# A GLA and stick-breaking hybrid layer: the first branch's output split where it is made, scores two blocks ahead, values one block behind, loads further ahead in the first pairs

## The chip, the cores and the metric

The kernel runs on one core of one Trainium2 chip, as one program. The metric is the device time of one execution in microseconds (us); the time before is the median of three executions, and a profile of one more execution shows where it goes. In the text PE is the matrix engine, PEld its weight loads, DVE the vector engine, ACT the scalar engine, POOL the GpSimd engine, and SP the engine whose queue issues nearly all DMAs.

## What is computed

One layer over 1024 tokens of width 1024, in float32. The reference, cut to what matters here:

```python
h = rmsnorm(x, norm_g)
proj = h @ w_in                                  # 9232 columns
(g_q, g_k, g_v, g_gate, g_rank, s_q, s_k, s_v, s_gate, m_logits) = jnp.split(proj, ...)
log_a = log_sigmoid(g_rank @ w_dec_up + b_dec) / 16
o_gla = gla_chunked(g_q, g_k, g_v, log_a)        # 4 heads, dk 128, dv 256
o_gla = rmsnorm(o_gla, gla_norm_g) * silu(g_gate)
y_a = o_gla @ w_pa
# stick-breaking, 8 heads, d 128, blocks of 128 queries against the causal prefix:
z = q @ k.T / sqrt(d); log1m = where(causal, log_sigmoid(-z), 0)
between = reverse_cumsum(log1m) - log1m
A = where(causal, exp(log_sigmoid(z) + between), 0);  o = A @ v
y_b = (o * silu(s_gate)) @ w_pb
x = x + (sigmoid_a * y_a + sigmoid_b * y_b) @ w_o;  return rmsnorm(x, final_g)
```

## The kernel before

Every product of float32 matrices is made of three matmuls of a reduced format (`F32R`): each operand is kept as a high part and a low part, and high x high, high x low and low x high are summed in PSUM. `split(src, hi, lo)` makes the parts: ACT copies `src` to `hi` (L161), DVE subtracts (L162). Arrays that a later stage needs go through DRAM (`d_...`).

The stages, in order: the norm of x and the first value projection; the other value projections; the **pairs stage**, in which `Pairs` runs 28 jobs of 7 units (12 matmuls of 512 columns each, a Strassen-like scheme) that project everything else but the second branch's gate; inside it, from unit 49 on, the **GLA stage**, which puts the first branch's small matmuls between the units; the **stick-breaking stage**; the projection of the second branch (`w_pb`) with the merge; and the output product.

*The first pairs.* In the first 22 units of `Pairs` the decay factors are made (`djobs`), in the next 27 (`tjobs`) the rows of `w_o` are loaded (`t_load`), combined by four subtractions on DVE (`t_sum`, L681) and stored (`t_store`, `d_t`). The recorded order of ACT and DVE is kept as written in the first 22 units (`manual_schedule`). In the other 27, and in the GLA and stick-breaking stages, a scheduler orders each engine's instructions by its own model of times. `gqk_pair` multiplies the GLA queries and keys with the decay factors `d_e`, which it loads (L523) at the moment of eviction.

*The GLA stage.* 32 steps (4 heads, 8 blocks of 128 tokens). `gl_gate` (L803) turns a block's output, multiplies it with its gate into `g` (two tiles of 128x128 side by side) and stores `g` in `d_ogl`, one array for each head.

*The stick-breaking stage.* `steps` are 8 heads of 8 blocks (h, i). `scores` (L878) multiplies a block's queries with the keys (`z`, up to 1024 columns in one or two PSUM banks, of which there are two), ACT makes two sigmoids of each bank (L898 into `eb`, L899 into `be`), DVE runs a product scan over the block on the diagonal (L902) and over the rest (L905) and multiplies (L910) into `be`. `turn` (L912) transposes `be` on PE, 128x128 at a time (L924), and splits the result into `ath`, `atl`. `values` (L929) multiplies two blocks' weights with the values (`av`, L940 to L942) in a single PSUM bank, multiplies with the gate (L943) and stores. The loop (L1018) does, for step s: load the queries of s + 2, load the next head's keys and values at i = 1, `scores` of s + 1, a unit of `st` if it stands there, `turn` of s, perhaps a unit, and `values` of the two blocks where i is odd. So PE meets `values` right behind the `turn` that it needs.

`st` is a line of units (24 matmuls of 512 columns each, `proj_t`, L200 to L202) that fill PE: three units a head (`SB_PLAN`), first the 16 units of the second branch's gate (`gate`), then the 16 of the first branch's output projection (`pa`). In between stands the reload of the first branch's output: `o_dma` loads 512 columns of one head of `d_ogl` into a `raw` tile (two buffers, which the weight loads use as well), and `o_split` splits them into `oq`, in the tiles that `hq` (the normed input) no longer needs. That is 16 `split`s of 128x512 on ACT and DVE, in two groups, in the fifth and sixth head.

All DMAs of these stages are issued by SP, in order; a DMA that has to wait for a buffer holds up those behind it.

Of the kernel before, what the change touches and what calls it, by code (L numbers as in the profile page):

```python
# [99 lines left out]
def hybrid_layer(ctx: ExitStack, tc: tile.TileContext, x, norm_g, w_in, w_up, b_dec,  # L100
# [20 lines left out]
    def dram_set(nm, count, shape, dt=F32):  # L121
        return [dram.tile(shape, dt, tag=f"{nm}{i}", name=f"d_{nm}{i}") for i in range(count)]
# [5 lines left out]
    d_gq, d_gk, d_e1, d_e2 = (dram_set(nm, GLA_H, [P, T]) for nm in ("gq", "gk", "e1", "e2"))  # L128
    d_gv = dram_set("gv", GLA_H, [P, NT, 2, DV])
    d_gg = dram_set("gg", GLA_H, [P, 2, T])  # L130
    d_ogl = dram_set("ogl", GLA_H, [P, 2, T])
    d_ga, d_gb, d_ma = (dram_set(nm, KB, [P, T]) for nm in ("ga", "gb", "ma"))
    d_a21 = dram_set("a21", 2, [P, 4, HALF])

# [29 lines left out]
    def half(n):  # L164
        return slice(n * HALF, (n + 1) * HALF)
# [57 lines left out]
        nc.gpsimd.tensor_tensor(r, r, nhalf, op=ALU.pow)  # L223


    def pair_job(w, c0, evict):

        t = {}

# [38 lines left out]
            nc.scalar.activation(t[nm], t[bank], AF.Copy)  # L268

        def unit(u):  # L270
            if u == 0:
                product("x", "B11", "A11", first=True)
                keep("s1", "x")
            elif u == 1:
                product("y", "B21", "A12", first=True)
                evict(0, 0, t["y"], t["s1"])
            elif u == 2:
                product("x", "T2", "S2")
                keep("s2", "x")
# [237 lines left out]
        return pair_job(w_in, c0 + i * DV, evict)  # L517

    def gqk_pair(c0, i, scale, d_e, dst):
        def evict(J, n, bank, add):  # L520
            h = 2 * i + J
            e = ev.tile([P, HALF], F32, tag="f", name="f")
            nc.sync.dma_start(e, d_e[h][:, half(n)])  # L523
            nc.vector.scalar_tensor_tensor(e, total(bank, add), scale, e, op0=ALU.mult, op1=ALU.mult)
            nc.sync.dma_start(dst[h][:, half(n)], e)

        return pair_job(w_in, c0 + i * DV, evict)

    def silu(v, dst):
        o = stage().bitcast(F32)  # L530
# [130 lines left out]
    for jobs in djobs:  # L661
        for fn, h in jobs:
            fn(h)
        pairs.run(1)
    manual.close()
    dq_ctx.close()


    wt = {}
    tq_ctx = ExitStack()  # L670
    tq = tq_ctx.enter_context(tc.tile_pool(name="tq", bufs=2, reuse_waits="tile"))

    def t_load(j):
        wt[j] = tq.tile([P, 4, HALF], F32, tag="t", name="t")
# [12 lines left out]
    for j in range(4):  # L687
        tjobs[5 * j].append((t_load, (j,)))
        for i in range(4):
            tjobs[5 * j + 4 + i].append((t_sum, (j, i)))  # L690
        tjobs[5 * j + 9].append((t_store, (j,)))
    for jobs in tjobs:
        pairs.run(1)
        for fn, args in jobs:
            fn(*args)
    tq_ctx.close()


# [104 lines left out]
    def gl_gate(h, b):  # L803
        t = gblk.pop((h, b))
        pt = ps.tile([P, HALF], F32, tag="tr", name="tr")
        for j in range(2):
            js = slice(j * P, (j + 1) * P)
            nc.tensor.transpose(pt[:, js], t["on"][:, js], ident)
        for j in range(2):
            js = slice(j * P, (j + 1) * P)  # L810
            nc.vector.scalar_tensor_tensor(t["g"][:, j], pt[:, js], vcol[:, 20 + j:21 + j], t["g"][:, j],
                                           op0=ALU.mult, op1=ALU.mult)
        nc.sync.dma_start(d_ogl[h][:, :, b * P:(b + 1) * P], t["g"])

    gl_half(0, 0)
    gl_load(*steps[0])
# [25 lines left out]
    def load_head(h):  # L842
        kts[h] = sl.tile([P, 2, T], F32R, tag="k", name="k")
        nc.sync.dma_start(kts[h].bitcast(F32), d_k[h])
        vts[h] = sl.tile([P, NT, 2, P], F32R, tag="v", name="v")
        nc.sync.dma_start(vts[h].bitcast(F32), d_v[h])

    def load_q(h, i):
        qts[h, i] = sl.tile([P, 2, P], F32R, tag="q", name="q", bufs=3)
# [1 line left out]

    steps = [(h, i) for h in range(SB_H) for i in range(NT)]
    load_head(0)
    for s in range(2):
        load_q(*steps[s])
    pairs.run()
    s_ctx.close()
# [13 lines left out]
    bets["first"] = sb.tile([P, T], F32, tag="be", name="be")  # L871
# [6 lines left out]
    def scores(h, i):  # L878
# [4 lines left out]
        om = ebuf[i % 2]  # L883
        be = bets.pop("first", None)
        if be is None:
            be = sb.tile([P, T], F32, tag="be", name="be")
        bets[h, i] = be
        npc = 1 if L <= HALF else 2
        w = L // npc
# [39 lines left out]
    def values(h, m):  # L929

        ath, atl = abuf[(m + 1) % 2]
        v = vts[h]
        gs = slice(m * DV, (m + 1) * DV)
        gate = ev.tile([P, HALF], F32, tag="f", name="f")[:, 0:DV]
        nc.sync.dma_start(gate, d_sg[h][:, gs])
        pav = ps.tile([P, HALF], F32, tag="av", name="av", bufs=1)
        ns = 2 * m + 2
        for s in range(ns):
            j = 2 * m + 1 - s
            nc.tensor.matmul(pav[:, 0:DV], v[:, j, 0], ath[:, s], start=s == 0, stop=False)  # L940
            nc.tensor.matmul(pav[:, 0:DV], v[:, j, 0], atl[:, s], start=False, stop=False)  # L941
            nc.tensor.matmul(pav[:, 0:DV], v[:, j, 1], ath[:, s], start=False, stop=s == ns - 1)  # L942
        nc.vector.tensor_mul(gate, pav[:, 0:DV], gate)  # L943
        nc.sync.dma_start(d_osb[h][:, gs], gate)

# [35 lines left out]
    def gate_load(h):  # L981
        return load(w_in, C_SG + h * P, ("g", h))
# [26 lines left out]
    line += [gate(5, 0), gate_load(7), gate(6, 0), o_dma(0, 0), gate(7, 0), o_dma(0, 1), o_split(0, 0), gate(5, 1),  # L1009
             o_dma(0, 2), o_split(0, 1), o_dma(0, 3), gate(6, 1), o_split(0, 2), pa_load(0), o_split(0, 3), pa_load(1),  # L1010
             gate(7, 1), o_dma(1, 0), pa_load(2), pa(0, 0), o_dma(1, 1), o_split(1, 0), o_dma(1, 2), pa(1, 0),
             o_split(1, 1), o_dma(1, 3), pa(2, 0), o_split(1, 2), o_split(1, 3)]
# [330 lines left out]
```

## Time and profile before

| what | us |
|---|---|
| median of 3 executions | 1249.28 (1249.15 to 1250.16) |
| the profiled execution | 1247.65 |
| its span, first to last instruction | 1245.8 |
| first pairs and decay, PE 74.66 busy | 125 to 200 |
| the stretch with the loads of `w_o`, PE 22.71 busy | 200 to 225 |
| GLA stage, PE 450.00 busy | 250 to 700 |
| stick-breaking stage, from its first score | 728 to 1028 |

A row of a view by lines names the source line, the engine, the operation, the output and the inputs, then the number of instructions, their busy time and the mean of one, and the idle time of the engine just ahead of them with what ended it. PE's busy time holds the tail of each matmul, since matmuls are pipelined: a row of 512 columns is shown with 0.39 us, while the next one starts 0.23 us later. How much PE does in a stretch is therefore read from starts, not from the busy share.

### The profile page before, as it was taken

The page shows a single profiled execution, that of the slowest core. Times are in us where ns is not written, and L with a number is a line of the kernel's source. Part 1 is how long each engine was busy: PE and PEld are TensorE (multiplying, and loading weights), DVE is VectorE, ACT ScalarE, POOL GpSimd, SP SyncE. Part 2 cuts the span into 40 slices and gives each one's busy share as a digit, 9 for nine tenths or more (in the row PEclk, how much of TensorE's full clock was granted, in tenths as well). Part 3 has the DMA queues.
Part 4 walks back from the last instruction along what each step waited for, and adds up shares of the span by engine and source line. Part 5 has one row for each costly group of instructions (what it writes and reads, how often), then busy time and mean ns, then how long its engine had stood idle before and what let it go on. Part 6 is the DMA issues. An engine that isn't in the chain of part 4 may idle for free. (4 is left out here: it accounts for less than half of the span.)

```text
span 1245.8 us, 17778 instructions
## 1 busy us (share of the span) xinstructions
PE 1214.7 (98%) x6339; PEld 1013.8 (81%) x6339; DVE 801.1 (64%) x1321; ACT 544.9 (44%) x1030; POOL 303.6 (24%) x304
## 2 busy tenths in 40 slices
PE   8999999999999999999999999999989999999997
PEld 8999887888888888888888887877777778888876
DVE  5475866746666576666744347787787876345576
ACT  5344663344334444444433334454554554332343
POOL 2495431414233232242232110000000000023201
PEclk9999999999999999999999999999999999999999
DMA  7554459836555465564643865354675535666653
GB/s 272 187 155 126 152 214 300 291 121 196 165 180 174 147 196 185 183 217 159 213 134 114 275 208 166 122 175 155 194 230 164 165 127 200 208 205 242 244 202 119
DMA packets 197460, 233.02 MB, mean 187 GB/s; under 512 B 12246, under 2 KB 143340, under 8 KB 194300
## 3 DMA queue, kind: packets, MB, share of 16 engines
q1 hardware_dynamic: 196796, 230.84, 56.3%
q8 instruction: 50, 0.82, 0.3%
q10 hardware_dynamic: 576, 1.05, 0.2%
q14 instruction: 38, 0.31, 0.1%
HBM read 145.34 MB, written 86.51 MB: 186 GB/s over the span
## 5 line engine op out<-in xcount | busy, mean ns | idle before, releaser
L299 DVE TENSOR_TENSOR f<-pp,f 128x512 f32<-128x512 f32 x84 | 57.9, 689 | 83.5 <-PE pp L264 80.7
L162 DVE TENSOR_TENSOR wl<-tt,wh 128x1024 fp32r<-128x1024 f32 x56 | 69.7, 1244 | 63.5 <-ACT wh L161 63.1
L162 DVE TENSOR_TENSOR wl<-raw,wh 128x1024 fp32r<-128x1024 f32 x55 | 79.6, 1448 | 37.0 <-ACT wh L161 35.9
L161 ACT ACTIVATE wh<-raw 128x1024 fp32r<-128x1024 f32 x55 | 58.0, 1057 | 89.2 <-PE pp L263 50.6
L161 ACT ACTIVATE wh<-tt 128x1024 fp32r<-128x1024 f32 x56 | 59.3, 1059 | 84.1 <-PE pp L263 83.6
L907 POOL TENSOR_SCALAR_AFFINE_SELECT be<-be 128x128 f32<-128x128 f32 x64 | 23.6, 369 | 280.6 <-ACT be L899 214.9
L236 POOL TENSOR_TENSOR tt<-raw 128x512 f32<-128x512 f32 x28 | 38.5, 1375 | 183.1 <-DVE wl L162 173.3
L268 ACT ACTIVATE f<-pp 128x512 f32<-128x512 f32 x84 | 49.6, 591 | 72.5 <-PE pp L264 67.5
L905 DVE TENSOR_TENSOR_SCAN eb<-eb 128x128 f32<-128x128 f32 (+6 forms) x56 | 71.8, 1282 | 6.3 <-ACT eb L898 4.0
L223 POOL TENSOR_TENSOR r<-r,nhalf 128x1 f32<-128x1 f32 x40 | 23.7, 593 | 207.8 <-DVE r L222 207.8
L898 ACT ACTIVATE eb<-z 128x384 f32<-128x384 f32 (+4 forms) x96 | 48.4, 505 | 41.7 <-PE z L896 28.4
L161 ACT ACTIVATE ath<-tr 128x512 fp32r<-128x512 f32 (+2 forms) x96 | 44.0, 496 | 37.2 <-PE tr L924 36.3
L162 DVE TENSOR_TENSOR atl<-tr,ath 128x512 fp32r<-128x512 f32 (+2 forms) x96 | 51.1, 546 | 6.6 <-ACT ath L161 6.6
L941 PE MATMUL av<-atl,v 128*128 128x256 f32 x160 | 46.9, 293 | 4.6 <-DVE atl L162 4.6
L200 PE MATMUL pp<-bh,wh 128*128 128x512 f32 x128 | 49.8, 389 | 0.0
L201 PE MATMUL pp<-bl,wh 128*128 128x512 f32 x128 | 49.8, 389 | 0.0
L202 PE MATMUL pp<-bh,wl 128*128 128x512 f32 x128 | 49.8, 389 | 0.0
L924 PE MATMUL tr<-ident,be 128*128 128x128 f32 x288 | 44.6, 278 | 5.2 <-DVE be L910 4.2
L910 DVE TENSOR_TENSOR be<-be,eb 128x128 f32<-128x128 f32 (+3 forms) x64 | 48.3, 755 | 2.1
L899 ACT ACTIVATE be<-z 128x384 f32<-128x384 f32 (+4 forms) x96 | 49.0, 512 | 0.0
L924 PEld LDWEIGHTS tr<-ident,be 128*128 128x128 f32 x288 | 32.8, 141 | 19.8 <-DVE be L910 9.9
L553 ACT ACTIVATE o<-o,vcol 128x512 f32<-128x512 f32 x32 | 23.2, 725 | 56.7 <-DMA o<-d_gb 40.8
(434 smaller groups left out, 4016.2 us busy)
## 6 DMA issues: line engine op xcount, KB each, us to landing
raw<-in_w_in_dram SPq DMA_DIRECT2D x31, 1024.0 KB, 6.0
d_v<-o SPq DMA_DIRECT2D x32, 256.0 KB, 3.0
d_gv<-o SPq DMA_DIRECT2D x32, 256.0 KB, 3.8
v<-d_gv SPq DMA_DIRECT2D x32, 256.0 KB, 3.1
d_q<-o SPq DMA_DIRECT2D x16, 512.0 KB, 3.9
d_k<-o SPq DMA_DIRECT2D x16, 512.0 KB, 5.1
k<-d_k SPq DMA_DIRECT2D x8, 1024.0 KB, 5.4
v<-d_v SPq DMA_DIRECT2D x8, 1024.0 KB, 7.5
```

The lines of the kernel that those rows point to most:

```text
L161: nc.scalar.activation(hi, src, AF.Copy)
L162: eng.tensor_sub(lo, src, hi.bitcast(F32))
L200: nc.tensor.matmul(pt, whi[:, kb], h_, start=kb == 0, stop=False)
L201: nc.tensor.matmul(pt, whi[:, kb], l_, start=False, stop=False)
L202: nc.tensor.matmul(pt, wlo[:, kb], h_, start=False, stop=kb == KB - 1)
L268: nc.scalar.activation(t[nm], t[bank], AF.Copy)
L299: nc.vector.tensor_add(add, bank, add)
L898: nc.scalar.activation(om[:, osl], zt[:, 0:w], AF.Sigmoid, scale=-inv_sqrt)
L899: nc.scalar.activation(be[:, osl], zt[:, 0:w], AF.Sigmoid, scale=inv_sqrt)
L905: nc.vector.tensor_tensor_scan(rest, rest, rest, om[:, T - P:T - P + 1], op0=ALU.mult, op1=ALU.min)
L910: nc.vector.tensor_mul(be[:, off:T], be[:, off:T], om[:, off + 1:T + 1])
L924: nc.tensor.transpose(pt[:, b * P:(b + 1) * P], be[:, c:c + P], ident)
```

## The change

1. `gl_gate` splits `g` as soon as it is made and stores both parts: `d_ogl` becomes two arrays, for the high and the low parts. `o_dma(n)` loads all four heads' 512 columns straight into `oq`, by four DMAs of 1 MB, and `o_split` is gone.
2. `scores` runs two blocks ahead of `turn` and not one; `be` has three buffers and not two; queries are loaded three steps ahead.
3. `values` of blocks 2m and 2m + 1 comes behind the `turn` of block 2m + 2, and the last of a head behind the first `turn` of the next.
4. A head's values are loaded as two halves; three halves fit (before, two heads).
5. In `tjobs` the sums stand two units later and the store too, with three buffers and not two; the decay factors of `gqk_pair` are loaded by `before(u)`, ahead of the unit's matmuls; the written order of ACT and DVE is kept up to the end of `tjobs`.

```diff
-    d_ogl = dram_set("ogl", GLA_H, [P, 2, T])
+    d_ogl = dram_set("ogl", 2, [P, 2, GLA_H, T])
...
         def unit(u):
+            if before:
+                before(u)
...
     def gqk_pair(c0, i, scale, d_e, dst):
+        es = {}
+
+        def before(u):
+            if u in (0, 3, 4, 5):
+                J, n = {0: (0, 0), 3: (1, 1), 4: (1, 0), 5: (0, 1)}[u]
+                es[J, n] = ev.tile([P, HALF], F32, tag="f", name="f")
+                nc.sync.dma_start(es[J, n], d_e[2 * i + J][:, half(n)])
+
         def evict(J, n, bank, add):
-            h = 2 * i + J
-            e = ev.tile([P, HALF], F32, tag="f", name="f")
-            nc.sync.dma_start(e, d_e[h][:, half(n)])
+            h, e = 2 * i + J, es.pop((J, n))
...
-    manual.close()
     dq_ctx.close()
...
-    tq = tq_ctx.enter_context(tc.tile_pool(name="tq", bufs=2, reuse_waits="tile"))
+    tq = tq_ctx.enter_context(tc.tile_pool(name="tq", bufs=3, reuse_waits="tile"))
...
         for i in range(4):
-            tjobs[5 * j + 4 + i].append((t_sum, (j, i)))
-        tjobs[5 * j + 9].append((t_store, (j,)))
+            tjobs[5 * j + 6 + i].append((t_sum, (j, i)))
+        tjobs[5 * j + 11].append((t_store, (j,)))
...
+    manual.close()
     tq_ctx.close()
...
-        nc.sync.dma_start(d_ogl[h][:, :, b * P:(b + 1) * P], t["g"])
+        o = stage()[:, :, 0:DV].rearrange("p s (e c) -> p s e c", e=2)
+        split(t["g"], o[:, 0], o[:, 1])
+        for e in range(2):
+            nc.sync.dma_start(d_ogl[e][:, :, h, b * P:(b + 1) * P], o[:, :, e].bitcast(F32))
...
-        vts[h] = sl.tile([P, NT, 2, P], F32R, tag="v", name="v")
-        nc.sync.dma_start(vts[h].bitcast(F32), d_v[h])
+        vts[h] = [sl.tile([P, NT // 2, 2, P], F32R, tag="v", name="v", bufs=3) for _ in range(2)]
+        for i, v in enumerate(vts[h]):
+            nc.sync.dma_start(v.bitcast(F32), d_v[h][:, 4 * i:4 * i + 4])
...
-    def o_dma(n, j):
-        return (lambda: reload_dma((d_ogl[j][:, 0], d_ogl[j][:, 1]), ("o", n, j), (n,)), False)
-
-    def o_split(n, j):
+    def o_dma(n):
+
         def go():
             for e in range(2):
-                if (n, e) not in oq:
-                    nm = f"a{n + 1}{e + 1}"
-                    oq[n, e] = quarter(a21b if nm == "a21" else hp, "o" + nm, nm)
-            reload_split(oq, ("o", n, j), j, (n,))
+                nm = f"a{n + 1}{e + 1}"
+                oq[n, e] = quarter(a21b if nm == "a21" else hp, "o" + nm, nm)
+                for i in range(2):
+                    nc.sync.dma_start(oq[n, e][i].bitcast(F32), d_ogl[e][:, i, :, half(n)])
...
-    scores(0, 0)
+
+    scores(*steps[0])
+    scores(*steps[1])
     for s, (h, i) in enumerate(steps):
-        if s + 2 < len(steps):
-            load_q(*steps[s + 2])
+        if s + 3 < len(steps):
+            load_q(*steps[s + 3])
         if i == 1 and h + 1 < SB_H:
             load_head(h + 1)
-        if s + 1 < len(steps):
-            scores(*steps[s + 1])
+        if s + 2 < len(steps):
+            scores(*steps[s + 2])
         st.run(SB_PLAN[i][0])
         turn(h, i)
         st.run(SB_PLAN[i][1])
-        if i % 2:
-            values(h, i // 2)
+        if i % 2 == 0 and s:
+            values(*((h, i // 2 - 1) if i else (h - 1, 3)))
+    values(SB_H - 1, 3)
```

How this moves instructions is seen at three places.

PE in the stick-breaking stage, in a head's sixth block, before: `z` are scores, `tr` the six transposes of block 5, `av` the values of blocks 4 and 5, `pp` a filling unit.

```order
L894 MATMUL z<-k,q 128x512
L895 MATMUL z<-k,q 128x512
L896 MATMUL z<-k,q 128x512
L924 MATMUL tr<-ident,be 128x128 x6
L894 MATMUL z<-k,q 128x512
L895 MATMUL z<-k,q 128x512
L940 MATMUL av<-ath_7206,v 128x256
L896 MATMUL z<-k,q 128x512
L201 MATMUL pp<-ha22l,wh 128x512
L202 MATMUL pp<-ha22h,wl 128x512
L200 MATMUL pp<-ha21h,wh 128x512
L941 MATMUL av<-atl_7207,v 128x256
```

The same six transposes in the changed program, with what stands around them on PE (`z` of 512 columns are block 7's scores, of 256 those of the next head's block 0).

```order
L955 MATMUL av<-ath_7334,v 128x256
L906 MATMUL z<-k,q 128x512
L907 MATMUL z<-k,q 128x512
L908 MATMUL z<-k,q 128x512
L936 MATMUL tr<-ident,be 128x128 x6
L906 MATMUL z<-k,q 128x256
L907 MATMUL z<-k,q 128x256
L908 MATMUL z<-k,q 128x256
L200 MATMUL pp<-ha11h,wh 128x512
```

The `av` of blocks 4 and 5 no longer stand behind these transposes; the last `av` ahead of the scores belongs to blocks 2 and 3. The weights of block 5, which the six transposes turn, come from scores that PE did a whole block earlier.

SP in the fifth head, before: `raw<-d_ogl` are reloads of the first branch's output, `q`, `k`, `v` the attention operands, `d_osb` the stored results.

```order
L533 DMA d_sg_107<-o 128x512
L953 DMA raw<-d_ogl_142 128x512 x2
L953 DMA raw<-d_ogl_143 128x512 x2
L177 DMA raw<-in_w_pa_dram 128x8x128
L533 DMA d_sg_105<-o 128x512
L177 DMA raw<-in_w_pa_dram 128x8x128
L944 DMA d_osb_111<-f 128x256
L846 DMA v<-d_v_97 128x2048
L850 DMA q<-d_q_80 128x2x128 x3
```

SP at the same place of the changed program, with the reload as four DMAs of 1 MB.

```order
L862 DMA q<-d_q_80 128x2x128
L1013 DMA oa11l<-d_ogl_140 128x4x512
L541 DMA d_sg_107<-o 128x512
L1013 DMA oa11h<-d_ogl_140 128x4x512
L1013 DMA oa12h<-d_ogl_141 128x4x512
L1013 DMA oa12l<-d_ogl_141 128x4x512
L858 DMA v<-d_v_96 128x1024
L957 DMA d_osb_111<-f 128x256
L541 DMA d_sg_105<-o 128x512
L957 DMA d_osb_111<-f 128x256
L862 DMA q<-d_q_80 128x2x128
L858 DMA v<-d_v_97 128x1024
```

Between two loads of queries there now stand 4 MB of the first branch's output, half a head of values and a store that waits for `values`. The loads of `w_pa` are no longer in this place: they were issued earlier.

DVE in the first pairs, before, with buffer numbers: `t_2289` is the third group of rows of `w_o`, `wl<-tt` a weight split that the next unit's matmuls need.

```order
L524 SCALAR_TENSOR_TENSOR f_2226<-f_2193,f_2226 128x512
L162 TENSOR_TENSOR wl_2233<-raw_2036,wh_2232 128x1024
L681 TENSOR_TENSOR t_2289<-t_2289 128x512 x2
L162 TENSOR_TENSOR wl_2268<-tt_2038,wh_2267 128x1024
L681 TENSOR_TENSOR t_2289<-t_2289 128x512
L299 TENSOR_TENSOR f_2263<-pp_2180,f_2263 128x512
```

The same place in the changed program; `t_2054` is the first group.

```order
L532 SCALAR_TENSOR_TENSOR f_2175<-f_2190,f_2175 128x512
L688 TENSOR_TENSOR t_2054<-t_2054 128x512
L162 TENSOR_TENSOR wl_2228<-raw_2033,wh_2227 128x1024
L688 TENSOR_TENSOR t_2054<-t_2054 128x512 x2
L162 TENSOR_TENSOR wl_2265<-tt_2035,wh_2264 128x1024
L301 TENSOR_TENSOR f_2261<-pp_2177,f_2261 128x512
```

Ahead of the same weight split DVE now has sums of rows that were loaded two groups earlier.

More of the change, by code (lines that the diff above doesn't have):

```diff
@@ L223, in rstd_of, with pair_job @@
         nc.gpsimd.tensor_tensor(r, r, nhalf, op=ALU.pow)
-    def pair_job(w, c0, evict):
+    def pair_job(w, c0, evict, before=None):
         t = {}
@@ L519, in gqk_pair @@
     def gqk_pair(c0, i, scale, d_e, dst):
+        es = {}
[4 more added lines that the diff above has]
+                nc.sync.dma_start(es[J, n], d_e[2 * i + J][:, half(n)])
         def evict(J, n, bank, add):
-            h = 2 * i + J
-            e = ev.tile([P, HALF], F32, tag="f", name="f")
-            nc.sync.dma_start(e, d_e[h][:, half(n)])
+            h, e = 2 * i + J, es.pop((J, n))
             nc.vector.scalar_tensor_tensor(e, total(bank, add), scale, e, op0=ALU.mult, op1=ALU.mult)
             nc.sync.dma_start(dst[h][:, half(n)], e)
-        return pair_job(w_in, c0 + i * DV, evict)
+        return pair_job(w_in, c0 + i * DV, evict, before)
     def silu(v, dst):
@@ L853, in hybrid_layer @@
     load_head(0)
-    for s in range(2):
+    for s in range(3):
         load_q(*steps[s])
@@ L870, in hybrid_layer @@
         nc.gpsimd.memset(e[:, T:T + 1], 1.0)
-    bets["first"] = sb.tile([P, T], F32, tag="be", name="be")
+    bets["first"] = sb.tile([P, T], F32, tag="be", name="be", bufs=3)
     abuf = [tuple(sb.tile([P, KB - 2 * i, 2 * P], F32R, tag=f"at{s}{i}", name=f"at{s}{i}", bufs=1)
@@ L885, in scores @@
         if be is None:
-            be = sb.tile([P, T], F32, tag="be", name="be")
+            be = sb.tile([P, T], F32, tag="be", name="be", bufs=3)
         bets[h, i] = be
@@ L939, in values @@
             j = 2 * m + 1 - s
-            nc.tensor.matmul(pav[:, 0:DV], v[:, j, 0], ath[:, s], start=s == 0, stop=False)
-            nc.tensor.matmul(pav[:, 0:DV], v[:, j, 0], atl[:, s], start=False, stop=False)
-            nc.tensor.matmul(pav[:, 0:DV], v[:, j, 1], ath[:, s], start=False, stop=s == ns - 1)
+            vh, vl = (v[j // 4][:, j % 4, e] for e in range(2))
+            nc.tensor.matmul(pav[:, 0:DV], vh, ath[:, s], start=s == 0, stop=False)
+            nc.tensor.matmul(pav[:, 0:DV], vh, atl[:, s], start=False, stop=False)
+            nc.tensor.matmul(pav[:, 0:DV], vl, ath[:, s], start=False, stop=s == ns - 1)
         nc.vector.tensor_mul(gate, pav[:, 0:DV], gate)
@@ L1008, in hybrid_layer @@
         line += [gate_load(h + 2), gate(h, 0), gate(h, 1)]
[L1009 to L1012, printed above, removed]
+    line += [gate(5, 0), gate_load(7), gate(6, 0), gate(7, 0), o_dma(0), gate(5, 1), pa_load(0), gate(6, 1), pa_load(1),
+             gate(7, 1), o_dma(1), pa_load(2), pa(0, 0), pa(1, 0), pa(2, 0)]
     for eb in range(KB):
```

## Prediction

> **What bounds the kernel now.** I read the busy line first, then PE's waits, then a table of windows, then start times in the timeline.
>
> ```profile
> PE 1214.7 (98%) x6339; PEld 1013.8 (81%) x6339; DVE 801.1 (64%) x1321; ACT 544.9 (44%) x1030; POOL 303.6 (24%) x304
> ```
>
> PE is the bound, but 98% overstates it: a matmul's record holds its tail. The waits of PE in the stick-breaking stage (761 to 1029 us):
>
> ```profile
> PE av L941 <- DVE atl L162: 4.3, 9, 0.7
> PE z L894 <- ACT be L899: 4.1, 2, 2.4
> PE tr L924 <- DVE be L910: 3.7, 12, 0.6
> PE av L940 <- ACT ath L161: 1.1, 1, 1.1
> PE z L894 <- DMA q<-d_q: 1.0, 2, 0.6
> ```
>
> These columns are total us, times, longest. PE waits for what DVE and ACT make of a block. Next, windows cut at the first score of each head (heads 2 to 7 of 8), and the GLA stage; the columns are length, then busy us and count of PE, PEld, DVE, ACT and POOL, PE's clock, the DMA share and GB/s:
>
> ```profile
> 761.10:798.70 37.60, 36.23 (x207) 29.49 (x205) 29.00 (x44) 18.24 (x43) 2.72 (x8) 1.00 0.53 165
> 798.70:836.70 38.00, 36.58 (x208) 29.45 (x205) 27.83 (x43) 17.86 (x41) 2.66 (x8) 1.00 0.45 146
> 836.70:874.00 37.30, 36.22 (x206) 29.46 (x204) 28.46 (x44) 17.92 (x43) 2.73 (x8) 1.00 0.46 149
> 874.00:914.90 40.90, 37.33 (x208) 31.05 (x206) 33.40 (x53) 22.91 (x50) 3.44 (x8) 0.96 0.64 200
> 914.90:955.70 40.80, 36.27 (x205) 29.55 (x204) 32.75 (x52) 22.77 (x51) 2.82 (x8) 1.00 0.67 219
> 955.70:994.20 38.50, 36.66 (x206) 29.42 (x205) 28.99 (x45) 19.64 (x42) 2.94 (x8) 1.00 0.47 151
> 250.00:700.00 450.00, 450.00 (x2234) 370.49 (x2233) 273.58 (x580) 189.89 (x385) 133.85 (x119) 1.00 0.54 174
> ```
>
> The GLA stage leaves PE no gap. A head takes 37.3 to 38.5 us, and the two heads with the reload 40.9 and 40.8. What would PE need alone? Its spacing, from the chain of waits (start, us, what):
>
> ```profile
> 962.33 0.23 PE pp L201
> 962.78 0.12 PE av L940
> 966.12 0.18 PE z L894
> 1034.35 0.44 PE tr L924 x4
> ```
>
> So 512 columns cost 0.227 us (three units of 24 matmuls in the table's heads go by that), 256 cost 0.12, 384 cost 0.18, a transpose 0.11. A head has 72 filling matmuls (16.3 us), scores of 4736 columns times three (6.3 to 6.4), 36 transposes (3.9) and 60 `av` (7.2): **33.9 us**. A quiet head loses about 3.7 us to this floor, a reload head 7. DVE is busy for 28 to 29 us of 37.6, so it is late by order, not by load.
>
> **The change, part by part.**
>
> *A, first pairs.* PE's one long stop there:
>
> ```profile
> 212.53 0.39 PE L264 MATMUL pp<-S4h,dl 128*128 128x512 f32 x1
> 215.20 0.50 PE L262 MATMUL pp<-ha22h,wh 128*128 128x512 f32 x1 [2.29 <-DVE f L299]
> 212.12 0.69 DVE L681 TENSOR_TENSOR t<-t 128x512 f32<-128x512 f32 x1 [2.83 <-DMA t<-in_w_o_dram]
> 212.73 1.22 DVE L162 TENSOR_TENSOR wl<-tt,wh 128x1024 fp32r<-128x1024 f32 x1
> 216.00:221.00 5.00, 5.00 (x16) 3.95 (x15) 4.17 (x7) 1.06 (x1) 0.00 (x0) 0.66 0.78 289
> ```
>
> DVE waits 2.83 us for rows of `w_o` with a weight split queued behind it, and PE starts 2.67 us after its last start: 2.44 us lost. Then 5 us run at 0.66 of the clock: 0.34 x 5 = 1.7 us more. Together 4.1. In the changed order the sums ahead of that split are of rows loaded two groups before, so the stop should go. What may come late in its place: ACT and DVE keep the written order to the end of `tjobs`, so the GLA stage's factors, and the queries behind SP's gate stores, come later than now; PE's first GLA scores could wait. Not shown in the trace; bounds 0 and the 2.4 us that the like wait above took, and I take 0.5, as 15 matmuls (3.4 us) stand ahead of those scores that did not before. The loads of `d_e` ahead of their units use the same buffers as the sums they feed; I take nothing, with 1 us either way. A = **-3.6**.
>
> [...]
>
> *B, the reload.* It takes from ACT and DVE sixteen splits:
>
> ```profile
> L161 ACT ACTIVATE oa11h<-raw 128x512 fp32r<-128x512 f32 x4 | 2.4, 628 | 7.8 <-PE pp L202 5.4 <-DMA raw<-d_ogl 2.3
> L162 DVE TENSOR_TENSOR oa11l<-raw,oa11h 128x512 fp32r<-128x512 f32 x4 | 2.7, 691 | 3.0 <-ACT oa11h L161 3.0
> ```
>
> that is 16 x 0.63 = 10 us of ACT and 16 x 0.69 = 11 of DVE. What counts is what they did to PE:
>
> ```profile
> 886.60 1.06 ACT L161 ACTIVATE wh<-raw 128x1024 fp32r<-128x1024 f32 x1 [2.86 <-DMA raw<-in_w_pa_dram]
> 888.26 0.50 PE L894 MATMUL z<-k,q 128*128 128x512 f32 x1 [2.40 <-ACT be L899]
> 888.50:893.00 4.50, 4.50 (x15) 3.52 (x15) 3.56 (x9) 1.94 (x5) 0.86 (x2) 0.62 1.03 377
> ```
>
> The reloads hold the `raw` buffers, so a weight of `w_pa` comes late, ACT stands before it with sigmoids behind it, and PE waits for a score bank; then the clock falls for 4.5 us. Both heads together lose 40.9 + 40.8 - 2 x 37.6 = 6.5 us to a quiet one. All of it goes; in its place stand four DMAs of 1 MB on SP, with queries behind them.
>
> ```profile
> q<-d_q SPq DMA_DIRECT2D x64, 128.0 KB, 3.1
> k<-d_k SPq DMA_DIRECT2D x8, 1024.0 KB, 5.4
> 966.66 0.28 SPq L846
> 967.03 7.70 DMA q<-d_q
> ```
>
> A queries' load lands in 3.1 us, and in 7.7 behind 1 MB of values. From 128 KB to 1 MB a load grows by 2.3 us, so 4 MB take 10.5 us by that slope, and about 14 at the 300 GB/s of the busiest slices. From the end of the unit that frees the buffers (`gate(7,0)`) to the scores that need the first late queries PE has: 7 transposes, 18 `av`, scores, 8 transposes, a unit, scores, 24 `av`: 0.8 + 2.2 + 0.4 + 0.9 + 5.4 + 0.6 + 2.9 = 13.2 us, and 5 us more up to the scores. It just fits; I take 1.5 us of waiting at each of the two reloads. B = -6.5 + 3 = **-3.5**; bounds -6.5, and +3 by the 14 us with the half head of values in line (2 us) and 3.1 to land.
>
> *C, scores two ahead and values one behind.* A quiet head's stops look like this:
>
> ```profile
> 863.70 0.39 PE L896 MATMUL z<-k,q 128*128 128x512 f32 x1
> 864.39 0.85 PE L924 MATMUL tr<-ident,be 128*128 128x128 f32 x6 [0.30 <-DVE be L910]
> 866.62 0.39 PE L200 MATMUL pp<-ha11h,wh 128*128 128x512 f32 x1
> 867.34 0.39 PE L941 MATMUL av<-atl,v 128*128 128x256 f32 x1 [0.33 <-DVE atl L162]
> ```
>
> From start to start 0.69 and 0.72 us where 0.227 is due: 0.46 and 0.49 lost. In this head six such stops (0.19, 0.31, 0.45, 0.46, 0.17, 0.49) make 2.1 of the 3.7 us; the rest are steps of about 0.1 us at matmuls that carry a wait, which the change leaves as they are. The 2.1 are just the two waits that it takes apart: transposes for the block's `be`, `av` for the parts of the transposes right ahead. In the changed order `be` of block 5 is needed after block 6's scores, a unit (5.4 us) and 12 `av`, and `av` of block 7 after the next head's transposes. What is late next: at blocks 2 and 3 there is little PE work between, and DVE has, ahead of the parts that `values(h, 0)` needs, a scan of 384:
>
> ```profile
> L905 DVE TENSOR_TENSOR_SCAN eb<-eb 128x384 f32<-128x384 f32 x1 | 1.0, 1008 | 0.0
> ```
>
> By the rows above about 0.3 to 0.5 us are left there, and some for a score bank, of which there still are two. I take 0.5 a head, that is -1.6, for eight heads (the reload heads have these stops beside their own): C = **-12.8**; bounds 0 and 8 x -2.8 (all but 0.9 of the 3.7).
>
> *D, the split in the GLA stage.* 32 more ACT and DVE instructions of 128x256, like these:
>
> ```profile
> L161 ACT ACTIVATE Ssh<-S 128x256 fp32r<-128x256 f32 x28 | 11.6, 414 | 2.1 <-DVE r L222 1.0 <-DVE S L792 0.6
> L162 DVE TENSOR_TENSOR Ssl<-S,Ssh 128x256 fp32r<-128x256 f32 x28 | 13.2, 473 | 1.4 <-ACT Ssh L161 1.2
> ```
>
> 13 us of ACT and 15 of DVE in 450 us, where they are busy for 190 and 274 and PE streams its units: cost 0. If that cover is gone each block pays up to 0.41 + 0.47, in all 28. Thirty-two more DMA issues and twice the bytes stored: SP waits for data nearly all the time; 0.
>
> *Sum.* -3.6 - 3.5 - 12.8 = -19.9 from the profiled 1247.65 us (its span and 1.85 around it): 1227.7. The median of the runs is 1.63 above the profiled execution, so **1229.4 us**.
>
> **Rivals.** *R1, nearly all of the stops go:* heads come to 34.8 us, the reloads cost nothing: A -4.1, B -6.5, C 8 x -2.8 = -22.4, in all -33: 1216. For it: DVE has 9 us of slack a head; against: its order is by a model that did not see today's stops either.
>
> *R2, the lead does nothing for the waits:* the scheduler fills PE less between blocks, since its model sees no wait, so new stops replace the old; C = 0 to -4, the rest as forecast: 1238 to 1242. For it: filling matmuls stand now in whole units, where before they were spread between scores and transposes.
>
> *R3, the queue:* queries wait for the whole 4 MB and the values behind; 5 us and a fall of the clock (1.7) at both reloads, 13 in place of 3: 1239. [...] Against it: only three loads of queries in each of two heads are behind.
>
> *R4, slower:* the GLA split is not hidden. `o` has three buffers, which the pairs' evictions use too; each split holds one until its stores land, evictions come late and PE's banks with them. It decides from 20 / 32 = 0.62 us a block; at the full 0.88 it gives 1229.4 + 28 = 1257. Against it: 450.00 of 450.00 and DVE at 61%.
>
> **How the numbers follow.** Forecast (1222 to 1235) 0.58, R1 0.15, R2 0.12, R3 0.08, R4 0.04, nothing to be seen 0.03. Range 1215 to 1241: it holds the forecast, R1, R3 and most of R2. About 2.5 us (0.2%) can be told from no change here. Faster: 0.58 + 0.15 + 0.12 + 0.08 = 0.93, of which I leave 0.02 to the same; so 0.91, same 0.04, slower 0.05.
>
> **What would show it.** A: no PE stop near 212 us and a clock of 1.0 from 200 to 250; no wait of L763 at the start of the GLA stage. B: heads 5 and 6 at 36 to 38 us, no `oa` split, a wait of scores for `q` of 1 to 2 us at each reload. C: quiet heads at 35.8 to 36.3 us, waits for `be` and `atl` down to a quarter. D: 250 to 700 still without a gap. Wrong it would be if heads stayed above 37, if PE waited for `q` in quiet heads too, or if PE stopped in the GLA stage.

## The result, and the profile after

| | us |
|---|---|
| before, median of 4 | 1249.22 (1245.67 to 1250.16) |
| changed, median of 4 | 1228.66 (1227.79 to 1230.13) |
| ratio, from all these runs (not quite that of the medians) | 0.9842, 95% interval 0.9819 to 0.9864 |
| changed, the profiled execution and its span | 1227.79 and 1225.9 |

The profiled execution is 19.86 us shorter than that of before; -19.9 was forecast. Whether the terms are right as well is another question, so the same views come again, now of the changed kernel. The busy line:

```profile
PE 1201.2 (98%) x6339; PEld 1016.3 (83%) x6339; DVE 802.5 (65%) x1337; ACT 543.6 (44%) x1046; POOL 320.4 (26%) x304
```

PE has the same number of instructions; the share has not moved, and again tells nothing. The table of windows, cut as before at the first score of heads 2 to 7, then the stretch of the `w_o` loads and the GLA stage (length, busy us and count of PE, PEld, DVE, ACT and POOL, clock, DMA share, GB/s):

```profile
749.50:785.61 36.11, 34.91 (x206) 30.20 (x205) 27.59 (x43) 17.88 (x41) 4.40 (x8) 1.00 0.55 166
785.61:821.46 35.85, 34.98 (x209) 30.23 (x207) 28.17 (x46) 17.22 (x41) 5.08 (x8) 1.00 0.49 158
821.46:857.42 35.96, 35.09 (x207) 30.22 (x206) 27.37 (x45) 17.25 (x42) 4.65 (x8) 1.00 0.48 155
857.42:894.90 37.48, 34.99 (x205) 30.08 (x205) 27.93 (x43) 18.16 (x42) 5.46 (x8) 1.00 0.82 272
894.90:932.54 37.64, 35.57 (x210) 30.40 (x209) 28.87 (x47) 19.45 (x44) 6.43 (x8) 1.00 0.85 280
932.54:967.97 35.43, 34.53 (x203) 30.09 (x202) 28.14 (x42) 18.03 (x41) 4.98 (x8) 1.00 0.63 207
200.00:250.00 50.00, 50.00 (x223) 41.37 (x222) 35.38 (x44) 16.65 (x22) 15.46 (x12) 1.00 0.74 243
250.00:700.00 450.00, 448.63 (x2227) 369.27 (x2226) 291.32 (x626) 198.56 (x417) 137.61 (x124) 1.00 0.60 191
```

Quiet heads take 35.9 to 36.1 us (37.3 to 38.0 before), the two with the reload 37.5 and 37.6 (40.9, 40.8). From 200 to 250 us there is no gap, and the clock is 1.00. The GLA stage now has one of 1.4 us. Third, the waits of PE in the stick-breaking stage (total us, times, longest):

```profile
PE tr L936 <- DVE atl L162: 8.1, 10, 1.8
PE av L954 <- DVE atl L162: 1.6, 6, 0.3
PE z L906 <- DMA q<-d_q: 0.4, 1, 0.4
PE tr L936 <- DVE be L922: 0.4, 2, 0.3
```

This is the surprise. The waits for `be` are down from 4.2 us (over the whole kernel before) to 0.4, and those of `av` from 5.7 (for `ath` and `atl`) to 1.6. But a wait that the profile of before does not list now leads: transposes waiting for `atl`, 8.1 us. A `turn` needs a PSUM bank, and a bank is free when the split of an older `turn` has read it. In the head from 785.61 (times of PE and DVE):

```profile
816.52 0.71 PE L936 MATMUL tr<-ident,be 128*128 128x128 f32 x5
817.61 1.82 DVE L917 TENSOR_TENSOR_SCAN eb<-eb 128x768 f32<-128x768 f32 x1 [0.45 <-ACT eb L910]
819.35 0.67 DVE L162 TENSOR_TENSOR atl<-tr,ath 128x512 fp32r<-128x512 f32 x1
819.93 1.08 DVE L922 TENSOR_TENSOR be<-be,eb 128x896 f32<-128x896 f32 x1
820.16 0.63 PE L936 MATMUL tr<-ident,be 128*128 128x128 f32 x4
820.93 0.28 DVE L162 TENSOR_TENSOR atl<-tr,ath 128x128 fp32r<-128x128 f32 x1
821.27 0.44 PE L936 MATMUL tr<-ident,be 128*128 128x128 f32 x2 [0.48 <-DVE atl L162]
```

The five transposes of block 4 fill two banks at 816.52. DVE takes the scan of block 6 (768 columns, 1.82 us) ahead of their splits, so the first bank is free at 820.0 and the second at 821.2; block 5's six transposes follow on PE behind only 12 `av` and six scores, and stop twice.

### The profile page after: what moved, and what is told of

It is laid out like the page before. It is cut to its first block, busy times and chain, and to the rows that moved or that the text cites. A ratio compares the mean times of both kernels' runs of the same rounds, so it can differ in the third digit from the quotient of the medians.

```text
span 1225.9 us, 17896 instructions
## 1 busy us (share of the span) xinstructions
PE 1201.2 (98%) x6339; PEld 1016.3 (83%) x6339; DVE 802.5 (65%) x1337; ACT 543.6 (44%) x1046; POOL 320.4 (26%) x304
## 4 chain that ended last, share of the span: by engine, by line
PE 69%; DVE 4%; DMA 2%; issue 2%; ACT 1%; SPq 0%; DVEq 0%; ACTq 0%
PE pp L262 11%; PE pp L264 11%; PE pp L263 11%; PE pp L202 7%; PE pp L201 7%; PE pp L200 7%; DVE eb L917 2%; PE tr L936 2%; PE xb L1212 1%; PE xb L1213 1%; PE xb L1214 1%; PE av L954 1%; PE av L955 1%; PE av L953 1%; DMA oa12l<-d_ogl 1%
## 5 line engine op out<-in xcount | busy, mean ns | idle before, releaser
L919 POOL TENSOR_SCALAR_AFFINE_SELECT be<-be 128x128 f32<-128x128 f32 x64 | 40.5, 636 | 245.8 <-ACT be L911 179.8
L162 DVE TENSOR_TENSOR wl<-raw,wh 128x1024 fp32r<-128x1024 f32 x55 | 76.4, 1390 | 42.1 <-ACT wh L161 41.0
```

The lines of the kernel that those rows point to most:

```text
L162: eng.tensor_sub(lo, src, hi.bitcast(F32))
```

## The experiments

Each group of kernels ran with the kernel before on the same chip; the ratio is to that. In the first four, one part alone is put on the kernel before.

**reload_alone**: the split in the GLA stage and the reload of two parts.

```diff
-        nc.sync.dma_start(d_ogl[h][:, :, b * P:(b + 1) * P], t["g"])
+        o = stage()[:, :, 0:DV].rearrange("p s (e c) -> p s e c", e=2)
+        split(t["g"], o[:, 0], o[:, 1])
+        for e in range(2):
+            nc.sync.dma_start(d_ogl[e][:, :, h, b * P:(b + 1) * P], o[:, :, e].bitcast(F32))
...
-    line += [gate(5, 0), gate_load(7), gate(6, 0), o_dma(0, 0), gate(7, 0), o_dma(0, 1), o_split(0, 0), gate(5, 1),
-             o_dma(0, 2), o_split(0, 1), o_dma(0, 3), gate(6, 1), o_split(0, 2), pa_load(0), o_split(0, 3), pa_load(1),
-             gate(7, 1), o_dma(1, 0), pa_load(2), pa(0, 0), o_dma(1, 1), o_split(1, 0), o_dma(1, 2), pa(1, 0),
-             o_split(1, 1), o_dma(1, 3), pa(2, 0), o_split(1, 2), o_split(1, 3)]
+    line += [gate(5, 0), gate_load(7), gate(6, 0), gate(7, 0), o_dma(0), gate(5, 1), pa_load(0), gate(6, 1), pa_load(1),
+             gate(7, 1), o_dma(1), pa_load(2), pa(0, 0), pa(1, 0), pa(2, 0)]
```

> The kernel before with only the first branch's output split where it is made and reloaded as two parts (terms B and D). By the terms: heads 5 and 6 lose the 2 x 3.2 us they have over a quiet head and get back what the queries behind the 4 MB cost; the whole is 3 to 5 us shorter (ratio 0.996 to 0.9976), the quiet heads stay at 37.3 to 38.5 us and 250 to 700 us keeps its 450.00 of 450.00. Rival, the split is paid for in the gated stage: that stage shows gaps and is 13 to 28 us longer, ratio 1.007 or more. Rival, with scores only one block ahead the late queries stop PE at each of the two reloads: heads 5 and 6 stay at 40 us, ratio 0.999 to 1.001, with waits of z for q of 2 us and more.

1241.06 us beside 1246.38, ratio 0.9959 (0.9945 to 0.9974): 5.1 us. Heads 5 and 6, and the GLA stage:

```profile
873.36:911.36 38.00, 35.83 (x207) 29.62 (x206) 29.16 (x44) 18.85 (x42) 3.19 (x8) 1.00 0.80 269
911.36:949.74 38.38, 36.22 (x207) 29.39 (x206) 27.09 (x43) 18.98 (x44) 3.24 (x8) 1.00 0.81 269
250.00:700.00 450.00, 450.00 (x2234) 370.29 (x2233) 287.17 (x612) 199.49 (x417) 134.42 (x119) 1.00 0.58 184
```

The two heads give back 5.3 of their 6.5 us, and PE waits for no queries there. The split in the GLA stage adds 13.6 us of DVE and 9.6 of ACT (273.58 and 189.89 before) and leaves PE without a gap: D is 0, and the rival of a split that isn't hidden falls.

**pairs_alone**: only the first pairs (third `tq` buffer, sums two units later, factors loaded by `before(u)`, `manual.close()` behind `tjobs`).

```diff
-            tjobs[5 * j + 4 + i].append((t_sum, (j, i)))
+            tjobs[5 * j + 6 + i].append((t_sum, (j, i)))
...
+    manual.close()
     tq_ctx.close()
```

> The kernel before with only the edits of the first pairs (term A). In the changed kernel the first score of the stick-breaking stage comes 2.65 us earlier. Theory that A adds to the rest: the stop near 212 us and the stretch at 0.66 of the clock behind it go, a wait of 1.4 us at the first scores of the gated stage comes, and the run is 2.5 to 3 us shorter, ratio about 0.998. Rival, the gain comes from elsewhere in the changed kernel (fewer DMA bytes beside it): the run is within 1 us of before, ratio 0.999 to 1.001.

1244.06 us beside 1246.38, ratio 0.9986 (0.9977 to 0.9995): 1.7 us, interval 0.6 to 2.9, where 2.5 to 3 was expected. In its profile the first score of the stick-breaking stage comes at 725.2 us, as in the changed kernel, not at 727.9. The fall of the clock near 216 us (1.7 us) need not be in every execution of the kernel before: its 21 executions in this group have a mean clock between 0.992 (1252.96 us) and 0.999 (1244.82 us), and one fall takes 0.0014 of the mean, so by this estimate some had none and some several. Its waits between 100 and 300 us hold the new one:

```profile
PE pa L763 <- POOL q L743: 1.4, 1, 1.4
```

**scores_alone**: scores two blocks ahead, `be` and queries to match. To fit, a head's values lie in two halves here too.

```diff
-        if s + 1 < len(steps):
-            scores(*steps[s + 1])
+        if s + 2 < len(steps):
+            scores(*steps[s + 2])
```

> The kernel before with scores two blocks ahead (three be buffers, queries three steps ahead), the values of a head in two halves as in the change, but the values right behind the turn of their block as before. Theory that the lead removes the waits of turns for be and of scores for their bank (1.8 and 0.5 to 1.2 us of a quiet head's 3.8), and leaves those of av for the parts (0.9): a quiet head loses 1 to 1.5 us, the run is 8 to 12 us shorter, ratio 0.990 to 0.994. Rival, the two shifts need one another: with a further scan ahead of the parts on DVE, av waits longer for atl than before, quiet heads stay at 37 us or more, ratio 0.997 to 1.003.

1242.96 us beside 1246.38, ratio 0.9975 (0.9964 to 0.9985): 3.1 us and not 8 to 12. Quiet heads take 37.5 to 38.2 us, no less than before. (Where the 3.1 us lie its profile does not tell: the profiled execution took 1245.48 us, the longest of the ten.) Its waits from 700 to 1030 us:

```profile
PE av L943 <- DVE atl L162: 11.2, 15, 1.1
PE tr L925 <- POOL be L908: 4.2, 7, 0.6
```

The rival was right: the wait of turns for DVE's `be` goes (0.7 us left, beside 4.2 for POOL's), and that of `av`, right behind its own `turn`, grows from 4.6 to 11.2.

**values_alone**: values one block behind, in halves; scores one ahead as before.

```diff
-        if i % 2:
-            values(h, i // 2)
+        if i % 2 == 0 and s:
+            values(*((h, i // 2 - 1) if i else (h - 1, 3)))
```

> The kernel before with values one block behind and the values of a head in two halves, scores one block ahead as before. Theory that only the waits of av go (0.9 us of a quiet head, 1.7 to 3.5 in heads 5 and 6): 4 to 8 us shorter, ratio 0.994 to 0.997, with the waits of tr for be as they were. Rival, the 12 to 24 av matmuls that stood between a turn and the next one's scores now stand elsewhere, so the turns wait longer for be: quiet heads at 37.5 us or more, ratio 0.998 to 1.004.

1234.65 us beside 1246.38, ratio 0.9908 (0.9891 to 0.9924): 11.5 us, above the 4 to 8 expected. Quiet heads and waits (700 to 1030 us):

```profile
757.55:793.97 36.42, 35.28 (x206) 30.07 (x205) 27.48 (x44) 17.48 (x40) 2.96 (x8) 1.00 0.55 170
793.97:830.48 36.51, 35.24 (x206) 30.10 (x205) 28.29 (x45) 18.62 (x41) 2.53 (x8) 1.00 0.49 152
PE tr L925 <- DVE be L911: 8.7, 14, 1.1
PE tr L925 <- DVE atl L162: 3.4, 4, 1.7
PE av L943 <- DVE atl L162: 1.0, 2, 0.5
```

So the later values alone are most of C: 1.3 us of the 1.7 that a quiet head saves. The waits for `be` do not go: in a quiet head PE's late starts at transposes add up to 1.6 us (1.5 before), and over the stage the listed waits for `be` grow from 4.2 to 8.7 us, as the rival said; the heads are shorter all the same. The lead of the scores, worth nothing to a quiet head by itself, takes another 0.4 once the values are out of the way. Of the 11.5 us, 1.8 lie ahead of the stage in the profile (first score at 726.1 us, not 727.9), in a place that the edit does not touch: there the stop near 213 us took 1.9 us and not 2.4, and the clock did not fall (the last section). The four ratios add up to -1.72%, the change has -1.58%: within their intervals the parts add.

The other six start from the changed kernel. It did not run on their chips; by its ratio it would stand at 1226.2 beside the first four and at 1227.0 beside the last two (turn_4, best), by the ratio's interval 2.8 us either way.

**turn_first**: at blocks 1 and 4 the `turn` stands ahead of the scores two blocks on.

```diff
-        if s + 2 < len(steps):
+        late = i in (1, 4)
+        if s + 2 < len(steps) and not late:
             scores(*steps[s + 2])
         st.run(SB_PLAN[i][0])
         turn(h, i)
+        if s + 2 < len(steps) and late:
+            scores(*steps[s + 2])
```

> The changed kernel, but at blocks 1 and 4 of a head the turn is written ahead of the scores two blocks on, so that DVE meets the splits of blocks 1 and 4 ahead of the scans of blocks 3 and 6. Theory that the changed kernel's new wait is one of order on DVE (the splits that free the transposes' banks stand behind a scan of 768 columns of 1.8 us): the waits of tr for atl (8.1 us in all, 1.2 a quiet head) nearly go, heads come to 34.7 to 35.2 us, the run is 6 to 9 us below the changed kernel, some 1220 beside its 1228.7. Rival, two banks for transposes are too few whatever the order: the wait stays or moves to block 6's transposes, heads at 35.6 us or more, within 2 us of the changed kernel. Rival, the turns now come too early for their be: waits of tr for be of 0.5 us a head and more take the gain.

1220.20 us beside 1245.91, ratio 0.9795 (0.9781 to 0.9810): 6.0 us below the changed kernel. Quiet heads 35.2 to 35.4 us.

```profile
PE tr L936 <- DVE be L922: 4.1, 7, 0.7
PE tr L936 <- DVE atl L162: 0.7, 1, 0.7
```

The wait for banks goes from 8.1 to 0.7: it was one of order on DVE, and two banks are enough. The third theory holds as well: block 3's `be` is now late at its `turn`, 0.8 us a head.

**turn_4**: only block 4's `turn` stands first (`late = i in (4,)`).

> The changed kernel with the turn of block 4 alone written ahead of the scores of block 6; block 1 stays as the change has it. Theory that one order on DVE (the splits of block 4 behind the scan of block 6) makes the waits of tr for atl, and that moving block 1 as well only made block 3's be late (the 0.8 us a head of tr for be that the run with both moved shows): the 1.15 us of a quiet head at the transposes go, the 0.55 us of av at block 2 stay, heads come to 34.8 to 35.0 us, the run is 7 to 9 us below the changed kernel and 1 to 3 below the run with both moved. Rival, the wait for be at the fourth turn is there whatever block 1 does: heads stay at 35.2 us or more, the same time as with both moved within 1 us.

1219.73 us beside 1246.65, ratio 0.9783 (0.9765 to 0.9801). Quiet heads 34.9 to 35.2 us, and the two waits of the last table are both small:

```profile
PE av L954 <- DVE atl L162: 1.6, 6, 0.3
PE tr L936 <- DVE atl L162: 1.0, 2, 0.7
PE tr L936 <- DVE be L922: 0.4, 2, 0.3
```

On DVE of the same head the splits now stand ahead of the scan, and block 5's six transposes run at one go at 817.76:

```profile
814.60 0.88 DVE L162 TENSOR_TENSOR atl<-tr,ath 128x512 fp32r<-128x512 f32 x2
816.01 1.82 DVE L917 TENSOR_TENSOR_SCAN eb<-eb 128x768 f32<-128x768 f32 x1 [0.21 <-ACT eb L910]
```

As a whole it cannot be told from the run with both blocks moved; the heads and waits can (0.3 us a head, and the wait for `be` from 4.1 to 0.4).

**q_four**: queries four steps ahead in four buffers.

```diff
-        if s + 3 < len(steps):
-            load_q(*steps[s + 3])
+        if s + 4 < len(steps):
+            load_q(*steps[s + 4])
```

> The changed kernel with queries loaded four steps ahead in four buffers instead of three in three. Theory that queries behind the 4 MB of the reload are what heads 5 and 6 still lose to a quiet head (1.5 and 1.7 us, as a wait of scores and then, through a late scan, as a longer wait of the transposes): both fall to 36 us, the run is 2.5 to 3.5 us shorter than the changed kernel. Rival, those two heads lose it on DVE and ACT, whose weight split and gate fall between two turns there: heads 5 and 6 stay at 37 us or more, the run within 1 us of the changed kernel.

1225.66 us beside 1245.91, ratio 0.9839 (0.9825 to 0.9854). As a whole that is not told from the changed kernel. Heads 5 and 6 are:

```profile
857.51:893.48 35.97, 34.78 (x205) 30.28 (x205) 27.66 (x43) 18.04 (x42) 4.36 (x8) 1.00 0.85 280
893.48:930.17 36.69, 35.54 (x209) 30.53 (x208) 28.43 (x47) 18.77 (x43) 5.10 (x8) 1.00 0.89 291
```

They give 1.5 and 0.95 us, and the profiled span is 2.3 shorter (1223.6): late queries are most of what these heads lost. How they were late is in the chain of waits of the changed kernel (start, us, what):

```profile
866.41 9.87 DMA oa12l<-d_ogl
...
878.47 0.46 SPq L858
...
878.99 5.89 DMA q<-d_q
...
885.02 0.41 PE z L906
...
891.97 1.82 DVE eb L917
893.79 0.59 DVE atl L162
...
894.52 0.63 PE tr L936 x4
```

and in SP's own waits between 866 and 884 us:

```profile
SPq L858 <- PE av L955: 8.1, 1, 8.1
```

Behind the 4 MB, SP stands for 8.1 us before the load of the second half of this head's values (L858), whose buffer the previous head's last `av` has to free. In a quiet head (from 821.46) two loads of queries go ahead of that half, 10.6 and 16.4 us into the head; here SP's order has them behind it, at 20.3 and 21.6 us (877.73 and 878.99), though the scores that free their own buffers had ended at 866.75 and 873.63. The second takes 5.9 us to land, the score starts 0.6 us late, a scan on DVE is late with it, and the transposes whose bank stands behind that scan wait 1.8 us.

**turn_first_q_four**: both edits of turn_first and q_four.

> The changed kernel with both edits, turns of blocks 1 and 4 ahead of the scores and queries four steps ahead. If both theories hold, 9 to 12 us below the changed kernel, some 1217 us, all heads at 35 us. If heads 5 and 6 lose by DVE's order alone, the same time as with the turns alone, within 1 us.

1220.56 us, ratio 0.9797 (0.9782 to 0.9811): no gain beside turn_first. With the turns first, heads 5 and 6 are at 35.4 and 37.4 us (35.3 and 36.2 without the fourth step); the sixth has two waits of scores for a bank, 1.4 us in all. Why there is not settled.

**close_old**: `manual.close()` back in its old place, the rest as changed.

```diff
         for fn, h in jobs:
             fn(h)
         pairs.run(1)
+    manual.close()
     dq_ctx.close()
...
-    manual.close()
     tq_ctx.close()
```

> The changed kernel with the written order of ACT and DVE given up where the kernel before gave it up (ahead of the sums of w_o); loads ahead, third buffer and later sums stay. DVE's sums then stand right behind their loads again, and the gated stage's first query is loaded ahead of the gates' stores. Theory that the written order is what removes the stop near 212 us and what makes the wait of 1.4 us at the gated stage's first scores: that wait goes, PE stops for 1.5 us or more near 200 to 230 us in its place, and the run is 1 to 3 us longer than the changed kernel. Rival, the third buffer and the earlier loads alone feed the sums in time: no stop, no wait, 1.5 us shorter than the changed kernel.

1228.93 us beside 1245.91, ratio 0.9864 (0.9848 to 0.9881), 2.7 above the changed kernel, which the two intervals do not tell apart. The stop at 212.6 us is back with 1.5 us, without a fall of the clock, and the wait at the gated stage is gone. That is a trade of equal stops: the first score of the stick-breaking stage comes at 725.5 us, beside 725.3 and the 727.9 of before. So what A gains by then comes from the third buffer, the later sums and the earlier loads, and the longer written order adds 0.2 us. Most of the 2.7 is head 6, which takes 39.5 us here, after a stop of 2.4 us and a fall of the clock (the last section). That the time came within the expected 1 to 3 us is therefore luck. What moved head 6, when the edit lies almost 700 us earlier, is not settled.

**best**: block 4's `turn` first, queries four ahead, and the GLA stage's first local products behind four units of the pairs.

```diff
     gl_load(*steps[0])
-    pairs.run(2)
+    pairs.run(4)
     gl_load(*steps[1])
     gl_local(*steps[0])
-    pairs.run(2)
```

> The changed kernel with block 4's turn first, queries four steps ahead, and the gated stage's first local scores written behind four units of the pairs instead of two, so that nine more matmuls (2 us) stand ahead of the wait of 1.4 us for its queries. If the waits add up: 1.5 us from the gated stage's start, 7 to 9 from the turns, 0.5 to 2 from heads 5 and 6, about 1216 to 1218 where the changed kernel is at 1226 on this chip. If the later local scores only push the same wait back, no gain beside block 4's turn alone.

1216.61 us beside 1246.65, ratio 0.9758 (0.9743 to 0.9773): about 10 us below the changed kernel, 3.1 below turn_4 on the same chip, and the shortest of all. Its waits of PE in the stick-breaking stage, all that the view lists:

```profile
PE av L953 <- DVE atl L162: 2.0, 7, 0.3
PE tr L935 <- DVE be L921: 0.3, 1, 0.3
```

The wait of 1.4 us at the GLA stage is gone (the first score of the stick-breaking stage comes at 723.9 us, 725.4 in turn_4), and heads 5 and 6 are at 35.2 and 35.4 (35.4 and 36.2 in turn_4).

## Why the forecast came true, and where it was wrong

The sum was right, 1228.66 for 1229.4, and so were three of four terms in size. The reasoning behind A, B and C was wrong in one step or more of each.

*A, -3.6 forecast.* The stop near 212 us and the fall of the clock behind it went, 4.2 us where 4.1 was forecast. But the price of the longer written order, set at 0.5, measured 1.5: I had counted the 15 matmuls that now stand ahead of the first local scores, and not how late SP and POOL begin with what those scores need. The step that failed is this choice within the bounds (0 to 2.4):

```profile
257.03 0.37 SPq L741 DMA_DIRECT2D qe<-d_gq  x1
262.56 0.23 POOL L715 MEMSET am<- 64x64 f32 x2
262.87 1.04 POOL L743 TENSOR_TENSOR q<-qe,fac 128x512 f32<-128x512 f32 x1
263.97 0.32 PE L763 MATMUL pa<-q,ke 128*64 128x128 f32 x1 [1.36 <-POOL q L743]
```

SP issues the queries behind a store of the gates, at 257.03, and they land 5.1 us later. POOL multiplies them at 262.87 and PE waits for it. What ends last ahead of POOL is its own work: from 256.06 on it runs four differences of weights, a mask (L711) and two clears (L715) without a pause, so in this order of POOL earlier queries alone would not have let it start sooner. By the first score of the stick-breaking stage the profile gains 2.7 us, beside the 3.6 forecast. best shows that what was missing was PE work ahead, less than 3 us of it (13 more matmuls stand between the issue of the queries and the first local scores).

*B, -3.5 forecast.* The sixteen splits' cost went (5.3 of 6.5 us alone). In the changed kernel the two heads lose 3.2 us to its quiet ones (37.48 + 37.64 - 2 x 35.97), where 3 was forecast: -3.3. The size is right, and late queries are most of the cause, as q_four shows (2.5 of the 3.2). The form is not: the wait of scores for `q` that I named as its sign is 0.4 us and not 1.5 twice; the lateness goes on through DVE's scan and PE shows it as a wait of transposes for a bank. And the queries are not held by the 4 MB alone: ahead of them SP waits for a buffer of the values. I had worked out the bytes in the queue, and not what the DMAs between them wait for.

*C, -12.8 forecast.* Heads 2 to 4 take 35.97 us on average where they took 37.66, -1.7 a head beside -1.6; the whole stage, from its first score to the first matmul of the output product, loses 17.1 us, of which 3.3 are B's, so C is -13.8. But three steps of its reasoning fell, and their errors cancel: that the size came out is in part luck. Late starts of PE in a quiet head, from the start times (due: 0.227 us for 512 columns and so on; early ones left out), mean of heads 2 to 4:

| | stops over 0.15 us | steps of 0.02 to 0.15 |
|---|---|---|
| before | 2.3 us | 1.9 us |
| changed | 1.6 | 1.1 |
| turn_4 | 0.6 | 1.1 |

I had 2.1 us of stops fall to 0.5, and the small steps stay. The stops fell to 1.6 only: "what is late next" I looked for at blocks 2 and 3, in `av` and in the score banks, and it came at block 5, in the transposes' banks, which the prediction does not name. The small steps fell by 0.8. Some are no costs of their own but the next step behind a stop (behind those of 0.49 and 0.53 us in the head from 798.7 it is 0.10 late too) and go with it, but these are 0.4 of the 1.9 us and make 0.2 of the 0.8. The other 0.6 are steps ahead of the scores (from 0.9 us to 0.3 a head), which values_alone has lost already; why, no run shows. And the two shifts do not each remove one wait: the lead alone moves the wait from `be` to `atl` (scores_alone), the later values alone bring most (values_alone).

*D, 0 forecast.* Right: reload_alone's GLA stage keeps 450.00 of 450.00.

Of the rivals, R1 (nearly all stops go, 1216) fell for the change, but best comes near it (0.9758 of 1249.28 is 1219), once an order on DVE, the lead of the queries and the start of the GLA stage are mended. What R2 feared, new stops for old, is the 8.1 us above; it cost less than R2's price. R3 is B's part, smaller. R4 fell.

## What to carry to other kernels

A shift that gives one engine more lead also puts more work into another engine's queue; ask for each buffer of the pipeline, PSUM banks too, whose instruction frees it and what now stands ahead of that instruction. When two shifts are made together, each alone shows which one earns; here one line moved (block 4's `turn` ahead of the scores) was worth another 7 us. A sum that comes true proves none of its terms: compare them one at a time.

## What the runs showed of the hardware

How long PE stopped, and what its clock did behind the stop. Two kernels that leave the first pairs as before, reload_alone and values_alone, stop at the same place (after the matmul at 212.99 and at 212.84 us), one for 2.29 us and the other for 1.94 beyond the 0.227 due; and close_old stops in head 6 for 2.42 us. The six us that follow each, in this order (the column behind the five engines is the clock):

```profile
215.30:221.30 6.00, 5.80 (x18) 4.64 (x19) 4.68 (x9) 1.06 (x1) 0.00 (x0) 0.72 0.77 266
214.70:220.70 6.00, 5.70 (x25) 4.70 (x26) 5.63 (x9) 1.06 (x1) 0.29 (x1) 1.00 0.90 278
894.40:900.40 6.00, 5.82 (x23) 4.90 (x24) 6.00 (x10) 1.43 (x4) 1.05 (x1) 0.72 0.88 290
```

A mean of 0.72 over six us is 1.7 us lost. In the kernel before, behind the stop of 2.44 us that ends at 215.20, the clock stands at half and then is full again (matmuls of 512 columns start 0.43 us apart in the first stretch, at 217.19, 217.62 and on, and 0.22 in the second, at 220.58 and 220.80):

```profile
217.00:220.00 3.00, 3.00 (x8) 2.32 (x8) 2.19 (x4) 0.82 (x1) 0.00 (x0) 0.50 0.88 318
220.50:225.00 4.50, 4.50 (x22) 3.69 (x21) 4.16 (x3) 0.60 (x1) 3.42 (x3) 1.00 0.84 213
```

In the kernels of this study, past their first 20 us, all six stops from 2.29 to 2.76 us (two of the kernel before, one each of reload_alone, pairs_alone, scores_alone and close_old) had 0.72 in the six us behind them, and the sixteen from 1.31 to 1.95 us had 1.00. The length of one stop does not tell all of it. values_alone has a seventh fall, somewhere from 700 to 1000 us:

```profile
700.00:1000.00 300.00, 286.35 (x1610) 243.62 (x1610) 221.77 (x348) 151.15 (x330) 24.43 (x69) 0.99 0.59 183
```

A fall of 1.7 us in 300 gives this 0.99 (the changed kernel has 1.00 over the same stretch), and the longest wait of PE that the view lists there is 1.7 us, by the table of values_alone. What else goes with a fall, no run shows. From the kernel before to values_alone the stop near 213 us is 0.5 us shorter (2.44 and 1.94), and the 1.7 us of the clock went with it in the two profiled executions; by the estimate at pairs_alone it need not in others.
